# The first stage of a two-layer hybrid block written out for four queues

## The chip, the cores and the metric

One NeuronCore of a Trainium2 chip. Its engines work side by side and each takes its own instructions in order: TensorE (PE: matmuls, with weight loads shown apart as PEld), VectorE (DVE), ScalarE (ACT), GpSimd (POOL) and SyncE (SP), which here issues most transfers from memory. Engines wait for one another through semaphores. The metric is the device time of one execution in microseconds (us).

## The reference, cut to what matters

Two layers over 256 latent tokens `lat` and 256 context tokens `cx`, width 1024. The change touches only the first stage: the modulation of layer 0, the norm, and the first three of the 22 hidden blocks of its first feed-forward network, for both streams.

```python
def _rms(t, g):
    t32 = t.astype(jnp.float32)
    y = t32 * lax.rsqrt(jnp.mean(t32 * t32, axis=-1, keepdims=True) + NORM_EPS)
    return y.astype(t.dtype) * g

def _modulate(t, g, shift, scale):
    return _rms(t, g) * (1 + scale) + shift

def _swiglu(h, w13, w2):
    gte, up = jnp.split(h @ w13, 2, axis=-1)
    return (jax.nn.silu(gte) * up) @ w2
...
    mod = (jax.nn.silu(c) @ mod_w[i] + mod_b[i]).reshape(bsz, 3, 3, 1, D_MODEL)
    modc = (jax.nn.silu(c_ctx) @ mod_w[i] + mod_b[i]).reshape(3, 3, D_MODEL)
    lat = lat + 0.5 * mod[:, 0, 2] * _swiglu(_modulate(lat, norm_g[i, 0], mod[:, 0, 0], mod[:, 0, 1]), ffn_w13[i, 0], ffn_w2[i, 0])
    if cx is not None:
        cx = cx + 0.5 * modc[0, 2] * _swiglu(_modulate(cx, norm_g[i, 0], modc[0, 0], modc[0, 1]), ffn_w13[i, 0], ffn_w2[i, 0])
```

Behind it come a short convolution and a second feed-forward network in layer 0, and a feed-forward network, attention and another feed-forward network in layer 1.

## The kernel before

Activations lie transposed: 8 tiles `k` of 128 features on the partitions, 512 tokens along the row (256 latent tokens as stream `s=0`, 256 context tokens as `s=1`). Each fp32 product is made of three: both operands are split into a high part (`hi`, type fp32r, by an ACT copy) and a rest (`lo`, by a DVE subtraction), and `mm3` adds hi x hi, hi x lo and lo x hi in PSUM. So each weight costs TensorE three matmuls, ACT a copy and DVE a subtraction.

A hidden block of w13 is a raw tile of 1 MB (`wr`, three buffers, filled by SyncE's queue), whose first half holds the up columns and whose second half the gate columns. `w13_mm` multiplies it with the normalised input `h` into two PSUM tiles, `pg` and `pu`; `w13_post` makes silu(gate) x up. The stage makes blocks 0, 1 and 2 side by side in six PSUM tiles, because the input comes in pairs of tiles `q` = 0..3: the shift (`ch` 0, `B00`) and scale (`ch` 1, `A00`) of each pair hang on a 1 MB load of modulation weights each. Their steps:

- `P ch q`, `mod_pe`: the load (also into a `wr` buffer), eight matmuls of 32 columns, and a copy `row` out of PSUM;
- `T ch q`, `mod_turn`: two tiny matmuls turn the row onto partitions, and DVE adds the bias into `A00` or `B00`;
- `N q`, `norm_q`: for each tile and stream, x times scale over rms (`scaled`, L256, DVE), plus shift into `hh` (L266, ACT) and, in fp32, into `h32` (L271, ACT), and the rest `hl` (L267, DVE);
- `M i q`, `w13_mm` for block `i` and pair `q`: 12 matmuls of 512 columns;
- `W i`: load and split of block `i`; `F` and the products at the start (`fill`): matmuls whose results nobody reads.

Ahead of this, `square_add` squares each tile of x on ACT and adds it to one sum per stream on DVE, and `rms_inv` turns the sums into 1/rms by matmuls with ones, a square root, a reciprocal and a matmul that spreads it over the partitions.

The order of TensorE's instructions in the stage is written out as a string; the other queues follow the planner's order, which may pull later work in between:

```python
FIRST_STEPS = (
    "P10 P00 T10 T00 F W0 N0 W1 M00 W2 M10 P11 M20 P01 T11 T01 N1 M01 P12 M11 P02 T12 T02 N2 "
    "M21 P13 M02 P03 T13 T03 N3 M12 M22 M03 M13 M23 S"
)
```

`S` loads silu of the conditioning, `scbc`. With it DVE makes the remaining modulation from here on, one unit at a time (`mod_unit`, L142): a unit is a product with a sum over the row, four units (two where one stream is enough) to a 1 MB load, which sits in a `wr` buffer too. `tick` strews these units over the later stages. `h32` feeds sums of blocks of the input (`FirstBlocks.sums`), which from the ninth hidden block on save one product in eight. `hop` is a pool of 16 buffers of 4 KB per partition; `h` takes eight of them (`Plain`), the split block sums eight more later.

Of the kernel before, what the change touches and what calls it, by code (L numbers as in the profile page):

```python
# [25 lines left out]
HEADS = 8  # L26
KVH = 2
EPS = 1e-6
WARM = 36
FILL = 12  # L30

FIRST_STEPS = (
    "P10 P00 T10 T00 F W0 N0 W1 M00 W2 M10 P11 M20 P01 T11 T01 N1 M01 P12 M11 P02 T12 T02 N2 "
    "M21 P13 M02 P03 T13 T03 N3 M12 M22 M03 M13 M23 S"
)


@with_exitstack
def hybrid_kernel(ctx: ExitStack, tc: tile.TileContext, a: dict, out: bass.AP):
# [20 lines left out]
    def psmall(s="pq"):  # L63
        return pss.tile([P, T2], F32, tag="sm", name=nm(s))
# [18 lines left out]

    sccol = const.tile([P, KT, 32], F32, name="sccol", tag="sccol")
    nc.vector.memset(sccol, 0.0)
    nc.scalar.activation(out=sccol[:, :, :2], in_=ccol, func=AF.Silu)

    rowsum = cload("rowsum", [P, 2])
    scbc = mp.tile([P, 2, D], F32, name="scbc", tag="scbc", bufs=1)

# [74 lines left out]
    jobs += [(1, ch, p) for ch in range(9) for p in range(4)]  # L165
    units = []
    owed = [0.0]

    def next_unit():
# [117 lines left out]
    def pick(h, k, c0, c1):  # L287
        return h.at(k, c0, c1)
# [322 lines left out]
    def ffn(l, b, h, tot, gate, tail, gs=(), ev=1.5):  # L611
        gs = list(gs)
        i0 = 0
        for t, n in enumerate(THIRDS):
            between = ()
            if tot == T2:
# [22 lines left out]
                for i in range(len(gs), n):  # L639
                    if t == 0 and not heads and i in AS_IS[l, b]:  # L640
# [77 lines left out]

    h = Plain()
    h32 = {}  # L720
    idle = psmall("idle")
# [6 lines left out]
    fill(idle, WARM)  # L728
    for k in range(KT):
        square_add(k, 0, T2)  # L730
    ris = []
    for s in range(2):
        ris.append(tp.tile([P, S], F32, name=nm("ris"), tag=f"ris{s}", bufs=1))
        nc.scalar.copy(ris[s], rms_inv(s, (accs[s], accs[s, "last"])))
# [3 lines left out]
    nc.vector.tensor_scalar(  # L738
        out=sb1, in0=modb[:, 0, KT : 2 * KT], scalar1=1.0, scalar2=None, op0=ALU.add
    )  # L740

    def both(t):
        return t.unsqueeze(2).to_broadcast([P, 2, 2])

    rows = {}

    def mod_pe(ch, q):


        raw = load_raw(a["mod0"][ch, q])  # L750
        pr = psmall("pr")
        for k in range(KT):
            g = 32 * (k % 4)
            nc.tensor.matmul(
                pr[g : g + 32, :S], sccol[:, k, :], raw[:, k * S : k * S + S],
                start=(k < 4), stop=(k >= 4), tile_position=(0, g),
            )
        row = tp.tile([P, S], F32, name=nm("row"), tag="t", bufs=3)
        nc.scalar.copy(row, pr[:, :S])
        rows[ch, q] = pr, row  # L760

    def mod_turn(ch, q):

        pr, row = rows[ch, q]
        for j in range(2):
# [8 lines left out]
            in1=both(sb1[:, k2] if ch else modb[:, 0, k2]),  # L774
            op=ALU.add,
        )

    def norm_q(q):
        k2 = slice(2 * q, 2 * q + 2)
        nc.vector.tensor_tensor(  # L780
            out=A00[:, k2, :], in0=A00[:, k2, :], in1=both(normg[:, 0, 0, k2]), op=ALU.mult
        )
        for k in range(2 * q, 2 * q + 2):
            for s in range(2):
                if (q, s) not in h32:
                    h32[q, s] = gp.tile([P, T2], F32, name=nm("hr"), tag="gl" if s else "gh")
                norm_k(s, k, h, A00, B00, ris[s], h32[q, s][:, (k % 2) * S : (k % 2) * S + S])

    pps = [(psum("pg"), psum("pu")) for _ in range(3)]

    ws, gs0 = {}, []

    def load_sc():
# [4 lines left out]
    def first_w(i):  # L798
        if i < 2:
            ws[i] = load_w(a["w13"][0, 0, i], fine=True)  # L800
            return
        raw = load_raw(a["w13"][0, 0, i])
        parts = [new_pair("w") for _ in range(4)]
        for j in (0, 2, 1, 3):
            split(*parts[j], raw[:, j * T2 : j * T2 + T2])
        ws[i] = lambda o: tuple(t[:, o % T2 : o % T2 + P] for t in parts[o // T2])

    steps = {
        "P": mod_pe,
        "T": mod_turn,  # L810
        "F": lambda: fill(pps[2][0], FILL),
        "S": load_sc,
        "W": first_w,
        "N": norm_q,
        "M": lambda i, q: w13_mm(pps[i], ws[i], h, range(2 * q, 2 * q + 2), 0, T2),
    }
    with tc.manual_schedule(engines={mybir.EngineType.PE}):
        for step in FIRST_STEPS.split():
            steps[step[0]](*(int(c) for c in step[1:]))
# [7 lines left out]
    qg = cload("qg", [P, 1])  # L827
    kg = cload("kg", [P, 1])
    cosT = cload("cosT", [P, S])
    sinT = cload("sinT", [P, S])  # L830


    hn = Plain()
# [517 lines left out]
```

## Time and profile before

| | us |
|---|---|
| median of three runs | 1587.46 (1584.85 to 1589.65) |
| the profiled execution | 1589.78 |
| its span, first to last instruction | 1588.0 |
| TensorE busy, of the span | 1565.0 (99%) |
| VectorE busy | 1319.8 (83%) |
| ScalarE busy | 738.2 (46%) |
| mean granted TensorE clock | 0.995 |

An engine is busy while it executes; waiting at a semaphore is idle. A busy TensorE need not run at full pace: matmuls overlap, so the distance from start to start says more than the length of one. The granted clock is the share of full speed that TensorE was given. In a timeline a row says start, length, engine, line, operation, output and inputs, and in brackets the idle time ahead of it and what ended it. A group's row says how often, busy time and mean length in ns, and the idle time ahead.

### The profile page before, as it was taken

What the parts mean: (1) busy time and instruction counts of PE and PEld (TensorE: products, weight loads), DVE (VectorE), ACT (ScalarE), POOL (GpSimd) and SP (SyncE); (2) the same over time, 40 slices, a digit from 0 to 9 for tenths busy, and PEclk for the clock granted to TensorE, in tenths of its full rate; (3) what the DMA queues carried; (4) which work ended last, traced back from release to release, by engine and by line L of the source; (5) the groups of instructions that cost most, each with busy time, mean ns of one, the idle gap of its engine ahead of it and who ended that gap; (6) DMA issues with size and microseconds to landing.
All of it is one profiled execution on the core that took longest, in us unless ns stands there. A gap on an engine that the chain in (4) does not pass through costs nothing.

```text
span 1588.0 us, 25040 instructions
## 1 busy us (share of the span) xinstructions
PE 1565.0 (99%) x10210; PEld 1423.9 (90%) x10210; DVE 1319.8 (83%) x2029; ACT 738.2 (46%) x1180; POOL 29.8 (2%) x20
## 2 busy tenths in 40 slices
PE   8999999999999999999999999999999999899998
PEld 6788998998888899989899899899899898888887
DVE  5778778879998879799798899898898899976654
ACT  5532452544322356335345375335255455655543
POOL 0000000000000000000000000000000005200000
PEclk9999999999999999999999999999999999999999
DMA  8545234234565412452342423443433654645552
GB/s 319 181 174 201 92 115 167 104 117 162 186 214 193 177 65 95 142 200 104 130 177 102 160 103 107 158 161 107 175 133 122 235 186 149 234 156 186 186 202 90
DMA packets 38419, 248.74 MB, mean 157 GB/s; under 512 B 5280, under 2 KB 7072, under 8 KB 11936
## 3 DMA queue, kind: packets, MB, share of 16 engines
q1 hardware_dynamic: 35712, 245.38, 43.5%
q10 hardware_dynamic: 2592, 1.76, 0.4%
q8 instruction: 80, 1.31, 0.3%
q14 instruction: 35, 0.29, 0.1%
HBM read 244.77 MB, written 1.05 MB: 155 GB/s over the span
## 4 chain that ended last, share of the span: by engine, by line
PE 93%; DVE 3%; ACT 2%; DMA 1%; issue 1%; POOL 0%; DVEq 0%; POOLq 0%; ACTq 0%
PE py L122 9%; PE py L123 9%; PE py L124 9%; PE p L124 7%; PE p L123 7%; PE p L122 7%; PE q L122 5%; PE q L123 5%; PE q L124 5%; PE py L1107 3%; PE pg L1107 2%; PE pu L1107 2%; PE pg L122 2%; PE pg L123 1%; PE pg L124 1%; PE pu L124 1%
## 5 line engine op out<-in xcount | busy, mean ns | idle before, releaser
L98 ACT ACTIVATE wh<-wr 128x1024 fp32r<-128x1024 f32 (+2 forms) x276 | 277.2, 1015 | 352.2 <-PE py L123 81.2
L99 DVE TENSOR_TENSOR wl<-wr,wh 128x1024 fp32r<-128x1024 f32 (+2 forms) x276 | 319.7, 1166 | 78.4 <-ACT wh L98 71.0
L142 DVE CUSTOM_DVE_ANT_0 junk<-wr,scbc,modb 128x1024 bf16<-128x1024 f32 x224 | 286.8, 1280 | 25.0 <-DMA wr<-in_modT 22.2
L123 PE MATMUL py<-gl,wh 128*128 128x512 f32 (+1 forms) x570 | 213.3, 374 | 0.0
L122 PE MATMUL py<-gh,wh 128*128 128x512 f32 (+1 forms) x570 | 213.3, 374 | 0.0
L124 PE MATMUL py<-gh,wl 128*128 128x512 f32 (+1 forms) x570 | 213.0, 374 | 0.0
L99 DVE TENSOR_TENSOR wl<-ws,wh 128x1024 fp32r<-128x1024 f32 x108 | 131.3, 1223 | 28.6 <-ACT wh L98 28.1
L98 ACT ACTIVATE wh<-ws 128x1024 fp32r<-128x1024 f32 x108 | 113.4, 1058 | 75.1 <-DVE ws L563 32.5
L124 PEld LDWEIGHTS py<-gh,wl 128*128 128x128 f32 x570 | 107.3, 188 | 19.1
L122 PEld LDWEIGHTS py<-gh,wh 128*128 128x128 f32 x570 | 107.4, 188 | 18.5
L123 PEld LDWEIGHTS py<-gl,wh 128*128 128x128 f32 x570 | 107.4, 188 | 18.2
L123 PE MATMUL p<-tl,wh 128*128 128x256 f32 x432 | 122.2, 283 | 0.0
L124 PE MATMUL p<-th,wl 128*128 128x256 f32 x432 | 122.2, 283 | 0.0
L122 PE MATMUL p<-th,wh 128*128 128x256 f32 x432 | 122.2, 283 | 0.0
L122 PE MATMUL q<-bh,wh 128*128 128x256 f32 x320 | 90.6, 283 | 0.0
L123 PE MATMUL q<-bl,wh 128*128 128x256 f32 x320 | 90.6, 283 | 0.0
L124 PE MATMUL q<-bh,wl 128*128 128x256 f32 x320 | 90.6, 283 | 0.0
L122 PEld LDWEIGHTS p<-th,wh 128*128 128x128 f32 x432 | 82.9, 192 | 0.3
L123 PEld LDWEIGHTS p<-tl,wh 128*128 128x128 f32 x432 | 82.9, 192 | 0.3
L124 PEld LDWEIGHTS p<-th,wl 128*128 128x128 f32 x432 | 82.9, 192 | 0.0
L446 DVE SCALAR_TENSOR_TENSOR x<-py,G,x 128x256 f32<-128x256 f32 x144 | 62.9, 477 | 6.3 <-PE py L124 6.0
L557 DVE TENSOR_TENSOR ws<-wr 128x1024 f32<-128x1024 f32 x54 | 65.7, 1218 | 0.0
(296 smaller groups left out, 4181.1 us busy)
## 6 DMA issues: line engine op xcount, KB each, us to landing
wr<-in_w SPq DMA_DIRECT2D x88, 1024.0 KB, 4.9
wr<-in_modT SPq DMA_DIRECT2D x64, 1024.0 KB, 4.8
wr<-in_w2b SPq DMA_DIRECT2D x24, 896.0 KB, 4.6
wr<-in_w2a SPq DMA_DIRECT2D x12, 1024.0 KB, 4.8
wr<-in_mod SPq DMA_DIRECT2D x8, 1024.0 KB, 6.1
wr<-in_cw_cx SPq DMA_DIRECT2D x8, 1024.0 KB, 4.8
wr<-in_w2l SPq DMA_DIRECT2D x8, 1024.0 KB, 4.8
wr<-in_cw_b SPq DMA_DIRECT2D x4, 1024.0 KB, 4.9
```

The source lines that it names most:

```text
L98: nc.scalar.activation(out=hi, in_=src, func=AF.Copy)
L99: nc.vector.tensor_tensor(out=lo, in0=src, in1=hi.bitcast(F32), op=ALU.subtract)
L122: nc.tensor.matmul(ps, wh, mh, start=first, stop=False, **kw)
L123: nc.tensor.matmul(ps, wh, ml, start=False, stop=False, **kw)
L124: nc.tensor.matmul(ps, wl, mh, start=False, stop=last, **kw)
L142: nc.vector.tensor_tensor_reduce(out=junk, in0=raw[:, j * D : j * D + D], in1=scbc[:, v, :], scale=1.0, scalar=modb[:, l, col : col + 1], ...
L446: nc.vector.scalar_tensor_tensor(out=x[:, m, s * S : s * S + S], in0=ps[:, o : o + S], scalar=g[:, m, s : s + 1], in1=x[:, m, s * S : s * ...
L557: tt(out=sm.rearrange("p (a b c) -> p a b c", a=2, b=2)[:, :, 0, :], in0=a21.unsqueeze(1).to_broadcast([P, 2, T2]), in1=self.raw[:, T2 : 3 ...
L1107: nc.tensor.matmul(ps, w[0], m, start=first, stop=False, skip_group_check=True)
```

## The change

- **Sums of squares.** Squares are made whole (512 columns) by DVE (tiles 0, 1, 7) and ACT (2 to 6), added in pairs on DVE, and the four pair sums go to a PSUM tile by matmuls with ones. One square root serves both streams. Its activation table, and that of silu ahead of it, is called by a one-column activation (`table`) at the start.
- **x over rms ahead.** `over_rms` makes x/rms of a pair of tiles on DVE into `h32`, ahead of the modulation. `norm_q` then has one ACT operation per tile and stream (scale and shift into `hh`), and two on DVE (the same in fp32, in place, and the rest). The multiplication by the norm's gain moves to `mod_turn`.
- **Raw modulation in operand buffers.** A modulation load goes to two `hop` buffers, not to a `wr` buffer.
- **Weights in two pieces.** Of each block's load the first piece holds the columns for input tiles 0 and 1 (256 of 1024 in each half), the second the other six tiles.
- **Four queues.** The order of TensorE, DVE, ACT and SyncE in the stage is written out, step by step, and the loads are issued apart from their use. Per weight the two products with the high part of the input come first (`products`).
- The filling matmuls are 18 and 5, not 36 and 12. Modulation units and block sums are tied to stand behind the last subtraction of the norm (`issue_after`). Five small loads for later stages go to SyncE's queue.

```diff
-WARM = 36
-FILL = 12
+WARM = 18
+FILL = 5
...
-        mod_unit(*units.pop(0))
+        with tc.issue_after(begun[-1].ins):
+            mod_unit(*units.pop(0))
...
-                            h.sums()
+                            with tc.issue_after(begun[-1].ins):
+                                h.sums()
...
+    def ask_mod(ch, q):
+        raws[ch, q] = [hot("mr", F32) for _ in range(2)]
+        for j, t in enumerate(raws[ch, q]):
+            nc.sync.dma_start(t, a["mod0"][ch, q][:, j * 1024 : j * 1024 + 1024])
+
+    def ask_w(i, part):
+        if part == 0:
+            ws[i] = wp.tile([P, 2048], F32, name=nm("wr"), tag="wr", bufs=3)
+        c = slice(0, S) if part == 0 else slice(S, 1024)
+        nc.sync.dma_start(
+            ws[i].rearrange("p (h c) -> p h c", h=2)[:, :, c],
+            a["w13"][0, 0, i].rearrange("p (h c) -> p h c", h=2)[:, :, c],
+        )
...
+    def over_rms(q, ri):
+        for s in range(2):
+            t = h32[q, s] = gp.tile([P, T2], F32, name=nm("hr"), tag="gl" if s else "gh")
+            nc.vector.tensor_tensor(
+                out=t.rearrange("p (k t) -> p k t", k=2),
+                in0=x[:, 2 * q : 2 * q + 2, s * S : s * S + S],
+                in1=ri[:, s * S : s * S + S].unsqueeze(1).to_broadcast([P, 2, S]), op=ALU.mult,
+            )
 
     def norm_q(q):
...
+        for j in range(2):
+            k = 2 * q + j
             for s in range(2):
...
+                hh, hl = pick(h, k, s * S, s * S + S)
+                t = h32[q, s][:, j * S : j * S + S]
+                g, b = A00[:, k, s : s + 1], B00[:, k, s : s + 1]
+                nc.scalar.activation(out=hh, in_=t, func=AF.Identity, scale=g, bias=b)
+                nc.vector.tensor_scalar(
+                    out=t, in0=t, scalar1=g, scalar2=b, op0=ALU.mult, op1=ALU.add
+                )
+                begun.append(
+                    nc.vector.tensor_tensor(out=hl, in0=t, in1=hh.bitcast(F32), op=ALU.subtract)
+                )
...
+    with tc.manual_schedule(engines=ORDERED):
+        for ch, q in ((1, 0), (0, 0)):
+            ask_mod(ch, q)
+        for i in range(3):
+            ask_w(i, 0)
+        table(AF.Silu)
+        nc.scalar.activation(out=sccol[:, :, :2], in_=ccol, func=AF.Silu)
+        table(AF.Sqrt)
...
+        ps = psum("ss")
+        fill(idle, WARM)
+        for k, eng in enumerate((nc.vector, nc.vector) + (nc.scalar,) * 5 + (nc.vector,)):
+            square(k, eng)
+            if k % 2:
+                pair_sum(k // 2)
+                token_sums(ps, k // 2)
+        rs = tp.tile([P, 4], F32, name="rs4", tag="rs4", bufs=1)
+        nc.scalar.activation(out=rs, in_=ps[:, :4], func=AF.Sqrt, scale=1.0 / D, bias=eps_t)
+        nc.vector.reciprocal(rs, rs)
+        mod_pe(1, 0)
+        rb = psum("rb")
+        for i in range(4):
+            nc.tensor.matmul(
+                rb[:, i * P : i * P + P], rs[:, i : i + 1].to_broadcast([P, P]), ident,
+                start=True, stop=True,
+            )
+        over_rms(0, rb)
+        ris = tp.tile([P, T2], F32, name="ris", tag="gm", bufs=3)
+        nc.scalar.copy(ris, rb)
+        mod_pe(0, 0)
+        w_hi(0, 0)
+        w_lo(0, 0)
+        mod_turn(1, 0)
+        mod_turn(0, 0)
+        pps[0] = psum("pg"), psum("pu")
+        pps[1] = psum("pg"), psum("pu")
+        fill(pps[1][0], FILL)
+        norm_q(0)
+        for ch, q in ((1, 1), (0, 1)):
+            ask_mod(ch, q)
+        products(0, 0)
+        for i in (1, 2):
+            w_hi(i, 0)
+        w_lo(1, 0)
+        over_rms(1, ris)
+        w_lo(2, 0)
+        for i in range(3):
+            ask_w(i, 1)
+        mod_pe(1, 1)
+        mod_pe(0, 1)
+        for ch, q in ((1, 2), (0, 2)):
+            ask_mod(ch, q)
+        products(1, 0)
+        w_hi(0, 1)
+        w_lo(0, 1)
+        mod_turn(1, 1)
+        mod_turn(0, 1)
+        w_hi(1, 1)
+        norm_q(1)
+        products(2, 0)
+        products(0, 1)
+        w_hi(2, 1)
+        w_lo(1, 1)
+        over_rms(2, ris)
+        mod_pe(1, 2)
+        products(1, 1)
...
+        norm_q(3)
+        products(2, 2)
+        for i in range(3):
+            products(i, 3)
...
-    convk = cload("convk", [P, 3, KT])
+    convk = cload("convk", [P, 3, KT], nc.sync)
```

The steps left out for the third and fourth pair follow the same pattern: `mod_pe` for scale and shift between products of earlier pairs, their turns, `over_rms`, `norm_q`, then the pair's products.

More of the change, by code (lines that the diff above doesn't have):

```diff
@@ L28 @@
 EPS = 1e-6
-WARM = 36
-FILL = 12
[L35 to L38, printed above, removed]
+WARM = 18
+FILL = 5
+ORDERED = {
+    getattr(mybir.EngineType, e) for e in ("PE", "DVE", "Activation", "SP")
+}
 @with_exitstack
@@ L726, in fill, with table, both @@
             nc.tensor.matmul(ps[:, :P], ones, ones, start=True, stop=True)
[L728 to L734, printed above, removed]
+    def table(f):
+        t = const.tile([P, 1], F32, name=nm("table"), tag="ready")
+        nc.scalar.activation(out=t, in_=eps_t, func=f)
+    def both(t):
+        return t.unsqueeze(2).to_broadcast([P, 2, 2])
     A00 = const.tile([P, KT, 2], F32, name="A00", tag="A00")
@@ new lines, in products @@
+    def products(i, q):
+        if i not in pps:
+            pps[i] = psum("pg"), psum("pu")
+        for k in (2 * q, 2 * q + 1):
+            hh, hl = pick(h, k, 0, T2)
+            w = [w_at(i, (1 - j) * 1024 + k * P) for j in range(2)]
+            for n in range(3):
+                for j in range(2):
+                    nc.tensor.matmul(
+                        pps[i][j], w[j][n == 1], hl if n == 2 else hh,
+                        start=k == 0 and n == 0, stop=k == KT - 1 and n == 2,
+                    )
@@ L796, in load_sc @@
             nc.scalar.activation(out=scbc[:, v, :], in_=scbc[:, v, :], func=AF.Silu)
[L798 to L819, printed above, removed]
+    gs0 = []
     done[0, 0] = done[0, 1] = 16
```

102 lines of the change are left out of this document (77 added, 25 removed).

## The prediction, made before the run

> **What bounds the kernel now.** I read the page first, then the busy time by stretches, then the first 75 us as a timeline, with the waits of each queue beside it.
>
> ```profile
> span 1588.0 us, 25040 instructions
> PE 1565.0 (99%) x10210; PEld 1423.9 (90%) x10210; DVE 1319.8 (83%) x2029; ACT 738.2 (46%) x1180; POOL 29.8 (2%) x20
> ```
>
> TensorE is busy nearly all the time, so a change is worth what it saves on TensorE's own queue. But a busy TensorE is not one at full pace, so I asked for stretches: the opening, the rest of the first stage, and the stretch behind it (columns: length, busy time of the engines with their instruction counts, granted clock, DMA share, GB/s).
>
> ```profile
> 0.00:22.30 22.30, 20.23 (x160) 17.78 (x160) 8.76 (x30) 11.68 (x23) 0.19 (x4) 0.92 0.90 321
> 22.30:72.00 49.70, 46.91 (x267) 33.37 (x268) 33.07 (x68) 32.30 (x64) 0.00 (x0) 0.97 0.63 232
> 72.00:126.00 54.00, 54.00 (x240) 44.72 (x239) 40.25 (x56) 14.63 (x20) 0.00 (x0) 1.00 0.51 181
> ```
>
> In the second stretch TensorE idles 2.8 us, its weight loads run 33 us of 50, the clock is below full and the DMA engines are free for a third of the time. Behind 72 us nothing of that is left. The timeline gives the ends of the stage: its first product, and the first product of the fourth weight block.
>
> ```profile
> 22.31 0.50 PE L122 MATMUL pg<-hh,wh 128*128 128x512 f32 x1
> ...
> 70.12 0.39 PE L122 MATMUL pg<-hh,wh 128*128 128x512 f32 x1
> ...
> 71.48 0.39 PE L122 MATMUL pg<-hh,wh 128*128 128x512 f32 x1
> ```
>
> Between the last two rows stand six matmuls: 0.227 us each at full pace. The stage has 3 blocks x 8 tiles x 6 = 144 products, 32.7 us. The rest of its TensorE work after 22.31 is six modulation products (`mod_pe`) and three pairs of turns (`mod_turn`):
>
> ```profile
> 51.40 0.39 PE L124 MATMUL pu<-hh,wl 128*128 128x512 f32 x1
> 51.71 1.07 PE L754 MATMUL pr<-wr,sccol 128*32 128x256 f32 x16
> 52.71 0.50 PE L122 MATMUL pg<-hh,wh 128*128 128x512 f32 x1
> ...
> 55.38 0.39 PE L124 MATMUL pu<-hh,wl 128*128 128x512 f32 x1
> 55.70 1.07 PE L754 MATMUL pr<-wr,sccol 128*32 128x256 f32 x16
> 56.70 1.21 PE L766 MATMUL pr<-rowsum,row 128*128 128x2 f32 x8
> 57.77 0.48 PE L122 MATMUL pg<-hh,wh 128*128 128x512 f32 x1
> ```
>
> A lone `mod_pe` costs 52.71 - 51.40 - 0.23 = 1.1, with the slow first product behind it 1.2. With a pair of turns it is 57.77 - 55.38 - 0.23 = 2.15, with that product 2.25, so a pair of turns is 1.05. Six and three make 7.2 + 3.2 = 10.4. The floor from first product to last is then 43.1 us; the trace takes 71.48 - 22.31 = 49.2. **6.1 us are lost inside the stage.** Where:
>
> ```profile
> 30.87 5.17 DMA wr<-in_mod
> ```
>
> ```profile
> L122 PE MATMUL pg<-hh,wh 128*128 128x512 f32 x25 | 11.0, 442 | 2.6 <-ACT hh L266 2.5
> ```
>
> ```profile
> 34.60:38.00 3.40, 1.39 (x16) 1.06 (x9) 2.19 (x8) 1.74 (x5) 0.00 (x0) 1.00 0.97 407
> 38.00:41.40 3.40, 3.36 (x7) 2.37 (x8) 2.34 (x5) 1.93 (x5) 0.00 (x0) 0.50 0.98 372
> 41.40:44.80 3.40, 3.40 (x27) 2.10 (x27) 0.00 (x0) 0.87 (x2) 0.00 (x0) 0.99 0.21 83
> ```
>
> ```profile
> SPq L94 <- DVE wl L99: 28.8, 5, 12.3
> SPq L94 <- PE pr L754: 20.1, 5, 7.5
> ```
>
> The first fence is a piece of the chain of waits: a modulation load issued at 30.87 holds it up to 36. TensorE waits for the normalised operand that hangs on it (2.5 us over the stage; second fence, groups of 22.3 to 72) and then runs a stretch at half clock (third fence): 1.7 us lost, since 3.4 us at 0.50 do 1.7 us of work. That leaves 1.9, mostly in the first products, whose operands trickle in. The last fence (SyncE's queue, 22.3 to 72) says why the load was late: SyncE waits for one of the three `wr` buffers. From 41.4 DMA has nothing to do, 83 GB/s.
>
> **The change, part by part.** *Buffers and loads.* Modulation halves go to the 16 `hop` buffers, of which `Plain` holds 8; four modulation loads fit in the other 8. The three weight blocks own the three `wr` buffers. SyncE's 49 us of waits for buffers thus go. What is next late: the transfer itself. Two modulation loads of before show its pace (issue row, then issue to landing):
>
> ```profile
> 6.71 0.81 SPq L94 DMA_DIRECT2D wr<-in_mod  x2
> DMA to landing us min/median/max: 6.7/7.7/8.8
> ```
>
> They land at about 13.4 and 16.0: 2.6 us for 1 MB, 403 GB/s, close to the 407 and 372 above. In all 2.1 MB of x, 8.4 of modulation and 3.1 of weights come in. In the new order of issue their bytes give: first two modulation loads at 13.0 and 15.7, first weight pieces 16.4 to 18, second pair 23, second weight pieces 25, 27 and 29, the last modulation load at 40. Small pieces have no row here; at the opening's mean of 321 GB/s the 13.6 MB and a start at 2 end at 45, the later bound.
>
> *Opening chain.* The rows of before (timeline, then groups of 22.3 to 72):
>
> ```profile
> 9.98 1.28 ACT L220 ACTIVATE sq<-x 128x512 f32<-128x512 f32 x2
> 11.62 1.28 ACT L242 ACT_TABLE_LOAD   x1 [0.36 <-issue]
> ...
> 13.43 1.88 PE L248 MATMUL ss<-ident,ri 128*128 128x128 f32 x8
> 15.24 3.04 PE L754 MATMUL pr<-wr,sccol 128*32 128x256 f32 x32
> ...
> 17.24 0.37 ACT L759 COPY row<-pr 128x256 f32<-128x256 f32 x1 [1.52 <-PE pr L754]
> ```
>
> ```profile
> L98 ACT ACTIVATE th<-hr 128x512 fp32r<-128x512 f32 x8 | 4.5, 617 | 0.0
> ```
>
> ```profile
> L372 DVE TENSOR_TENSOR hr<-hr,hr 128x512 f32<-128x512 f32 x2 | 1.4, 692 | 0.0
> ```
>
> ```profile
> L266 ACT ACTIVATE hh<-t,mod 128x256 fp32r<-128x256 f32 x14 | 7.0, 497 | 4.0 <-DVE mod L771 4.0
> ```
>
> The last quarter of x is there at 9.98. Squares 6 and 7 now run side by side, a square and a pair sum by 0.69: 11.4; token sums, root (its table loaded ahead, where ACT waits for x) and reciprocal: 12.8. The first modulation load lets `mod_pe` start at 13.0; at half clock it takes 1.5 (half of 3.04): 14.5. Spreading the reciprocals (`rb`, as the 1.88 row): 16.4; the second `mod_pe` 17.9; row copy 0.37: 18.3. ACT then splits the first weight piece, two cuts of 256 columns at about 0.4 (row copy), DVE follows 0.4 later: 19.5. This is new in front of the modulation adds, which DVE has queued behind it; the three small adds 20.0; two operands on ACT by 0.5: **first product at 21.0 instead of 22.3, 1.3 earlier.** x over rms is two products of 0.69 on DVE, 16.4 to 17.8, under the second `mod_pe`; without that cover it costs 1.4.
>
> The table-load row says 1.28 us, of which I count 0.5 as saved, as the token sums ran beneath it. The Trainium skill, "ScalarE: Activation LUTs", section "What ACT_TABLE_LOAD costs", gives 2.66 us for a switch with its drain; by it the gain would be some 1.4 larger, but the root starts right behind the 1.28 here.
>
> *Norm.* Per tile and stream before: two ACT operations and two on DVE. Now one on ACT, two on DVE, one of them a scale-and-shift of 256 without a row; I take 0.3 (nearest: half of the 0.692 row, which has twice the columns and two tensors), bounds 0.15 and 0.5, times four per pair of tiles. ACT's `hh` has two pointers now: the 0.497 row to 0.6. It sits behind DVE's splits and `over_rms` in the written order, so I followed all queues through: with weights at 25, 27 and 29 the second norm starts behind its turns at 30, and its operands are there 2 us before their products; the third and fourth have 1 to 2 us. So inside the stage I put these at nothing: two other blocks' products (2.7 each) cover each. Without the cover a pair costs its 2 to 3 us.
>
> *Loads moved from ACT's queue to SyncE's* (`convk` to `sinT`): used hundreds of us later, nothing. *`issue_after`*: operand sums and modulation units may no longer enter DVE before the last norm; see the third case.
>
> *The clock.* Fewer filling products: 18 and 5 for 36 and 12. What idling does:
>
> ```profile
> 7.00:10.70 3.70, 3.68 (x33) 3.49 (x32) 3.44 (x11) 3.62 (x8) 0.00 (x0) 1.00 1.03 321
> 10.70:14.10 3.40, 2.51 (x21) 2.37 (x21) 1.50 (x6) 2.37 (x4) 0.00 (x0) 1.00 1.02 403
> 14.10:17.50 3.40, 3.40 (x29) 2.03 (x32) 0.00 (x0) 1.00 (x3) 0.00 (x0) 0.50 0.98 386
> ```
>
> A thinly used stretch is followed by one at 0.50, here and at 38.0. With the fill ending near 6.5 the half rate comes earlier in the opening, so I counted the opening at half clock; and another may fall on the first products. I take off 1.1 for two thirds of a stretch (0 to 3.4).
>
> **Sum.** 1.3 + 6.1 - 1.1 = 6.3 us earlier at the fourth block, and behind it TensorE is full, so it is kept. The profiled execution took 1589.78 (span 1588.0), 2.3 above the median; 1587.5 - 6.3 gives **1581**. About 0.3%, 4.8 us, is what a measurement of this kernel tells from no change.
>
> **Rivals.** *The clock and the opening eat it.* Were the opening no earlier and two stretches of the first products at half clock, 6.1 - 3.4 = 2.7 remain: 1585. For it: fewer fills, a longer written chain with in-order queues. Against: half clock never follows a full stretch. The Trainium skill, "TensorE: Matmul & The Clock Gate", Part 1, says the same: half rate after an idle window of about 3.4 us, windows running freely. By that rule this change loses at its thin opening; the rows agree (0.50 over 3.4 us, twice).
>
> *Slower: DVE behind the stage.*
>
> ```profile
> 70.00:80.00 10.00, 10.00 (x46) 8.29 (x45) 9.93 (x15) 3.45 (x5) 0.00 (x0) 1.00 0.51 179
> ```
>
> ```profile
> L99 DVE TENSOR_TENSOR tl<-hr,th 128x512 fp32r<-128x512 f32 x8 | 5.1, 682 | 0.0
> ```
>
> ```profile
> 75.39 1.21 DVE L99 TENSOR_TENSOR wl<-wr,wh 128x1024 fp32r<-128x1024 f32 x1
> 76.52 1.28 DVE L142 CUSTOM_DVE_ANT_0 junk<-wr,scbc,modb 128x1024 bf16<-128x1024 f32 x1
> ...
> 104.56 1.23 DVE L99 TENSOR_TENSOR wl<-wr,wh 128x1024 fp32r<-128x1024 f32 x1 [4.10 <-ACT wh L98]
> ```
>
> DVE is full after the stage (first row). Eight splits of operand sums (second) and eight sums of 0.69 ran before 72; now all wait for the last norm, and about half, some 5 us, is added to that backlog. The idle 4.1 at 104 and its like absorb it, if weight splits come first. If a load's four modulation units (5.2) stand ahead of a split that the next block needs, TensorE waits up to 5.2 per block, five blocks. Slower from the second block on (6.3 / 5.2), by over 0.3% from the third: 1581 + 15.6 = 1597. Against: at 75.39 the split stands before the units.
>
> *The change does not do what it says*, products still waiting for loads: at 240 GB/s the last load lands at 57 where 51 is wanted; no gain, 1587. The rows against: 321 to 407.
>
> **Numbers.** Forecast 0.60. The clock case 0.17 and the loads 0.08, both within 0.3%: 0.25. DVE 0.15. Range: 1576 (no half clock, the opening 2 us better, spread of the runs) to 1590, into the two middle cases; the DVE case lies outside.
>
> **What would show it.** First product near 21; the fourth block's first near 65; no SyncE waits on `wl` or `pr` in the stage; DMA full to 40; at most one half-clock stretch after the first product; TensorE full from 65 to 126. Wrong, if half clock reaches past 28, if TensorE waits for ACT `hh` over 1 us, or if weights of the fourth to eighth block are awaited.

## The result, and the profile after

| | before | after |
|---|---|---|
| median of 8 runs each, same chip (us) | 1587.36 (1584.85 to 1589.65) | 1581.99 (1578.61 to 1583.59) |
| the profiled execution (us) | 1589.78 | 1582.34 |
| its span (us) | 1588.0 | 1580.5 |
| first product of the stage | 22.31 | 21.82 |
| first product of the fourth block | 71.48 | 66.12 |

After over before is 0.9963, 95% interval 0.9952 to 0.9975: 5.4 us faster by the medians, where 6.3 were forecast. The two profiled spans differ by 7.5; of that, 5.4 stand at the fourth block, 5.2 at the first product with the second weights (`py`, 120.7 for 125.9), 5.0 at 1264 (its last product there, 1264.4 for 1269.4), and 7.5 at the end. The last 2 us come and go in stages that the change doesn't touch, and the medians don't have them: from that last product to the end the traces of all fourteen kernels here take between 315.0 and 318.6 us, without order by the edits.

The first line of the page of after and its engines' busy time:

```profile
span 1580.5 us, 24959 instructions
PE 1558.3 (99%) x10176; PEld 1422.0 (90%) x10176; DVE 1322.6 (84%) x2031; ACT 731.5 (46%) x1163; POOL 29.7 (2%) x20
```

6.7 of the 7.5 us by which the spans differ are gone from TensorE's busy time: a matmul at half clock is busy too. The stretches of after (length, busy time of PE, PEld, DVE, ACT, POOL with counts, granted clock, DMA share, GB/s):

```profile
6.40:9.80 3.40, 2.55 (x23) 2.36 (x22) 3.20 (x6) 2.58 (x6) 0.00 (x0) 1.00 1.01 324
9.80:13.20 3.40, 2.79 (x28) 2.69 (x31) 1.45 (x3) 0.63 (x1) 0.00 (x0) 1.00 1.01 387
13.20:16.60 3.40, 3.40 (x24) 2.17 (x24) 0.18 (x1) 0.64 (x2) 0.00 (x0) 0.50 1.07 362
16.60:20.00 3.40, 2.61 (x29) 1.82 (x28) 1.75 (x4) 1.48 (x4) 0.00 (x0) 0.99 0.88 254
20.00:23.40 3.40, 3.40 (x14) 2.88 (x13) 2.59 (x10) 2.72 (x7) 0.00 (x0) 0.51 0.99 253
...
24.40:40.00 15.60, 15.21 (x105) 10.77 (x104) 11.27 (x26) 7.91 (x15) 0.00 (x0) 1.00 1.02 404
40.00:66.00 26.00, 25.98 (x155) 19.63 (x154) 16.28 (x37) 13.60 (x22) 0.00 (x0) 1.00 0.46 189
66.00:126.00 60.00, 60.00 (x266) 49.53 (x265) 51.62 (x75) 21.88 (x31) 0.00 (x0) 1.00 0.50 178
```

The wait and the half-clock stretch between 34 and 41 are gone: from 24.4 on the clock is full and TensorE idles 0.4 us. DMA is full until 40. What is left of half clock lies in the opening (13.2 to 16.7) and on the first products (20.0 to 23.5). SyncE's waits from 22.3 to 72, and its timeline from 22 on:

```profile
SPq L91 <- DVE wl L96: 34.1, 2, 23.8
```

```profile
22.59 11.05 SPq L743 DMA_DIRECT2D mr<-in_mod  x8
34.54 1.61 SPq L970 DMA_DIRECT2D scbc<-in_c  x2
37.15 1.62 SPq L91 DMA_DIRECT2D wr<-in_w  x2
```

The last modulation loads go out in one run, and none waits for `pr`. SyncE still waits long for `wl`, but for the buffers of later blocks, behind every load of the stage. TensorE's timeline of after, from the token sums to the fifth block:

```profile
12.16 1.05 PE L797 MATMUL ss<-ones,sq 128*128 128x1 f32 x8 [0.61 <-DVE sq L793]
13.14 1.91 PE L810 MATMUL pr<-mr,sccol 128*32 128x256 f32 x16
...
16.85 1.07 PE L810 MATMUL pr<-mr,sccol 128*32 128x256 f32 x16
...
19.25 0.61 PE L822 MATMUL pr<-rowsum,row 128*128 128x2 f32 x4 [0.79 <-ACT row L815]
...
21.82 0.79 PE L870 MATMUL pg<-hh,wh 128*128 128x512 f32 x1
...
25.51 1.50 PE L810 MATMUL pr<-mr,sccol 128*32 128x256 f32 x24
27.40 0.64 PE L810 MATMUL pr<-mr,sccol 128*32 128x256 f32 x8 [0.39 <-DMA mr<-in_mod]
...
66.12 0.39 PE L119 MATMUL pg<-hh,wh 128*128 128x512 f32 x1
...
77.14 0.39 PE L119 MATMUL pg<-hh,wh 128*128 128x512 f32 x1
```

From first product to fourth block it is 44.3 us where the floor is 43.1. The first 12 products take 25.51 - 21.82 = 3.7 instead of 2.7 (half clock), and one modulation load is awaited for 0.39. Together these 1.4 are more than the loss of 1.2, so the floor was a little too high. And 49.2 - 44.3 = 4.9 of the 5.4 come from inside the stage, 0.5 from the opening.

### The profile page after: what moved, and what is told of

Same layout as the page of the kernel before. It is cut to its first block, busy times and chain, and to the rows that moved or that the text cites. A ratio compares the mean times of both kernels' runs of the same rounds, so it can differ in the third digit from the quotient of the medians.

```text
span 1580.5 us, 24959 instructions
## 1 busy us (share of the span) xinstructions
PE 1558.3 (99%) x10176; PEld 1422.0 (90%) x10176; DVE 1322.6 (84%) x2031; ACT 731.5 (46%) x1163; POOL 29.7 (2%) x20
## 3 DMA queue, kind: packets, MB, share of 16 engines
q8 instruction: 79, 1.29, 0.3%
HBM read 244.77 MB, written 1.05 MB: 156 GB/s over the span
## 4 chain that ended last, share of the span: by engine, by line
PE 92%; DVE 2%; DMA 2%; ACT 2%; issue 0%; POOL 0%; SPq 0%; ACTq 0%; DVEq 0%; POOLq 0%
PE py L119 9%; PE py L120 9%; PE py L121 9%; PE p L121 7%; PE p L120 7%; PE p L119 7%; PE q L119 5%; PE q L121 5%; PE q L120 5%; PE py L1260 3%; PE pg L1260 2%; PE pu L1260 2%; PE py L1261 1%; PE pg L121 1%; PE pu L121 1%; PE pg L119 1%
## 5 line engine op out<-in xcount | busy, mean ns | idle before, releaser
L95 ACT ACTIVATE wh<-wr 128x1024 fp32r<-128x1024 f32 (+2 forms) x264 | 270.6, 1033 | 340.3 <-PE py L120 85.1
L96 DVE TENSOR_TENSOR wl<-wr,wh 128x1024 fp32r<-128x1024 f32 (+2 forms) x264 | 312.4, 1189 | 71.0 <-ACT wh L95 63.5
## 6 DMA issues: line engine op xcount, KB each, us to landing
mr<-in_mod SPq DMA_DIRECT2D x16, 512.0 KB, 10.2
```

The costliest lines, as they stand in the source:

```text
L95: nc.scalar.activation(out=hi, in_=src, func=AF.Copy)
L96: nc.vector.tensor_tensor(out=lo, in0=src, in1=hi.bitcast(F32), op=ALU.subtract)
```

## Experiments

Each was timed in five rounds against the kernel before on the same chip, whose median was 1588.14 us beside the first four kernels, 1587.94 beside the next four and 1587.57 beside the last four; across these groups the ratios are compared (0.001 is 1.6 us), not the medians. The first two rows repeat the result. The "4th block" is its first product in that kernel's trace. "Half clock" gives the stretches of the first 75 us, in steps of 0.1 us, in which that trace shows a granted clock of about 0.5. The expectations name their theories by letters; where a letter matters, the text says what it stands for.

| kernel | median us | ratio to before (95%) | first product | 4th block | half clock |
|---|---|---|---|---|---|
| before | 1587.36 | 1 | 22.31 | 71.48 | 14.1 to 17.6, 38.0 to 41.5 |
| after | 1581.99 | 0.9963 (0.9952 to 0.9975) | 21.82 | 66.12 | 13.2 to 16.7, 20.0 to 23.5 |
| buffers only | 1588.87 | 1.0007 (0.9999 to 1.0016) | 21.66 | 72.57 | 37.2 to 44.1 |
| order only | 1588.19 | 0.9999 (0.9987 to 1.0011) | 22.17 | 72.67 | 33.7 to 40.6 |
| buffers and order | 1584.69 | 0.9980 (0.9970 to 0.9991) | 21.86 | 67.84 | none |
| two loads ahead | 1583.00 | 0.9965 (0.9951 to 0.9979) | 21.60 | 65.02 | 11.1 to 18.1 |
| weights whole | 1585.46 | 0.9984 (0.9974 to 0.9995) | 21.84 | 68.37 | 11.8 to 18.7, 22.1 to 25.6 |
| late small loads | 1581.72 | 0.9967 (0.9957 to 0.9977) | 22.27 | 65.90 | 10.2 to 17.1, 20.4 to 23.9 |
| opening reordered | 1580.61 | 0.9956 (0.9944 to 0.9968) | 21.67 | 65.10 | 11.5 to 18.5 |
| fills as before | 1584.35 | 0.9980 (0.9969 to 0.9990) | 23.55 | 66.47 | 16.3 to 19.8 |
| no table calls | 1582.94 | 0.9968 (0.9957 to 0.9979) | 21.91 | 65.33 | 12.0 to 19.0 |
| no tie | 1582.16 | 0.9967 (0.9954 to 0.9980) | 22.16 | 65.54 | 10.9 to 17.9 |
| DVE loaded | 1591.40 | 1.0025 (1.0014 to 1.0035) | 23.29 | 66.66 | 12.6 to 19.6 |
| opening and late small loads | 1580.42 | 0.9956 (0.9942 to 0.9970) | 21.31 | 64.74 | 10.9 to 17.8 |

Each place in a trace is that of one execution. After, two loads ahead, no tie and DVE loaded have the same opening, and their first products lie between 21.60 and 23.29; so a first product that is some tenths of a us earlier shows nothing by itself. The time from the first product to the fourth block is steadier.

**Buffers only.** The prediction put the wait at 36 down to the shared `wr` buffers. So the kernel before, with nothing but its modulation loads moved:

```diff
-        raw = load_raw(a["mod0"][ch, q])
+        raw = [hot("mr", F32) for _ in range(2)]
+        for j, t in enumerate(raw):
+            nc.sync.dma_start(t, a["mod0"][ch, q][:, j * 1024 : j * 1024 + 1024])
...
```

> The kernel before with one edit: a raw modulation load goes to two operand buffers, not to a weight buffer. Theory A (three shared buffers held the loads back, and that is most of the gain): the modulation wait at 36 (2.0 us) and the half-clock stretch behind it (1.7 us) go, the fourth block's first product comes at about 67.8 instead of 71.5, the median falls by 3.7 us to about 1583.7. Rival B (the written order of the queues makes the gain, more buffers alone do not): the fourth block stays at 71 or later, the median within 1 us of 1587.4.

Nothing was gained. TensorE's timeline of this kernel, then ACT's:

```profile
37.91 0.79 PE L122 MATMUL pg<-hh,wh 128*128 128x512 f32 x1 [2.96 <-ACT hh L266]
```

```profile
34.32 1.28 ACT L798 ACT_TABLE_LOAD   x1
35.61 1.06 ACT L798 ACTIVATE scbc<-scbc 128x1024 f32<-128x1024 f32 x1
36.57 0.49 ACT L266 ACTIVATE hh<-t,mod 128x256 fp32r<-128x256 f32 x1
```

The loads were early and SyncE's waits on `pr` gone, and TensorE still waited 2.96 for `hh`. With the loads out of the way the planner pulled the silu of the conditioning, with its table load, ahead of `hh`. That cost about 1.0 of the 2.96: the shift was ready at 35.57 (a DVE row of 35.42, 0.15 us long), and `hh` began at 36.57. But even without that the norm could not have been ready, as DVE's timeline of before shows:

```profile
35.48 0.16 DVE L771 TENSOR_TENSOR A<-pr,sb 128x4 f32<-128x4 f32 x1 [4.63 <-PE pr L766]
36.04 0.48 DVE L256 SCALAR_TENSOR_TENSOR t<-x,A,ris 128x256 f32<-128x256 f32 x1 [0.20 <-DMA wr<-in_mod]
```

The chain of waits of before names the load for 5.17 us, yet the idle time that ended with it is 0.20. What came last are the turns, then three steps (add, scale, `hh`) while TensorE has nothing left: in the old string `T11 T01 N1` are followed at once by `M01`, which needs them.

**Order only, and both together.** So the second theory: the wait is the latency of the norm behind its turns. One edit of the string puts another block's products there; the second kernel has both edits.

```diff
-    "... M10 P11 M20 P01 T11 T01 N1 M01 ..."
+    "... M10 P11 P01 T11 T01 N1 M20 M01 ..."
```

> The kernel before with TensorE's written order alone changed at one place: the third block's first products (M20) stand behind the second pair's turns, so that they cover the norm. New theory F (the wait at 36 was the norm's latency with nothing of TensorE behind the turns, and the loads' lateness stood hidden below it: order and buffers are needed together): P01 moves ahead of M20, from 33.8 to about 31, where its load is not there before 33.5; the wait moves there, the fourth block's first product stays at 71 to 72, median 1587 to 1588. Rival G (order is the whole of it): 68, median 1584.

> The kernel before with that order and the raw modulation in operand buffers. Theory F: the loads are early (in the run with buffers alone both land before 30) and the norm lies under M20; the wait of 2 to 3 us and the half-clock stretch (1.7 us) go, the fourth block's first product comes at 67.0 to 68.5 instead of 71.5, median 1583.5 to 1584.5, two thirds of the whole change. Rival H (neither counts; the gain of the change comes from ACT's and DVE's written order): 70 or later, median above 1586.

Order alone gains nothing either; its TensorE timeline shows the wait one step earlier, now at the load, and its stretch from 34 to 42 the half clock:

```profile
33.17 1.41 PE L754 MATMUL pr<-wr,sccol 128*32 128x256 f32 x16 [2.42 <-DMA wr<-in_mod]
```

```profile
34.00:42.00 8.00, 8.00 (x32) 6.31 (x25) 4.53 (x12) 3.68 (x9) 0.00 (x0) 0.59 0.91 356
```

The same stretch with the buffers only:

```profile
34.00:42.00 8.00, 5.04 (x17) 3.77 (x17) 4.61 (x12) 6.77 (x12) 0.00 (x0) 0.70 1.03 413
```

With both, the timeline and the same stretch read:

```profile
30.85 0.64 PE L756 MATMUL pr<-mr,sccol 128*32 128x256 f32 x8 [0.35 <-DMA mr<-in_mod]
...
36.30 0.50 PE L123 MATMUL pg<-hl,wh 128*128 128x512 f32 x1 [0.21 <-DVE hl L267]
```

```profile
34.00:42.00 8.00, 7.68 (x43) 5.03 (x42) 2.99 (x7) 4.86 (x11) 0.00 (x0) 1.00 1.03 410
```

Two waits lay one upon the other: singly 0.7 and 0.2 us above before (both within the measurement), together 3.2 below. That is the larger half of the change's 5.4, and it is shown. The clock makes it look sharper than the waits alone: behind its wait each single edit runs at half clock for 6.9 us, before for 3.5, and both together not at all. The longer stretch costs up to 1.7 us; less that, each alone would start the fourth block at about 70.9, some 0.5 ahead of before (an estimate from the table), and both together start it 3.6 ahead. Whether a single edit always has the longer stretch, one trace of each doesn't show. The rest, 67.84 to 66.12, can be read from the two traces and was not run by itself: with both edits the first 24 products take 29.00 - 21.86 = 7.1 us where 24 x 0.227 is 5.4, as `hh`, weights and their rests trickle in; in after 12 products go first, then the modulation products, and the next 12 don't stall.

**Two loads ahead.** Is it the depth of four loads that counts? Here four `hop` buffers of after are held idle until the last scale add, so that only two modulation loads fit.

```diff
+    held = [hot("held", F32) for _ in range(4)]
+    for t in held:
+        nc.gpsimd.memset(t[:, :2], 0.0)
...
+    for t in held:
+        nc.gpsimd.tensor_copy(out=t[:, :2], in_=A00[:, KT - 1, :])
```

> The changed kernel with four of the sixteen operand buffers held by an idle tile until the last modulation add, so that two modulation loads fit at a time, not four. Theory A': what counts is that modulation no longer competes with weights for buffers, not the depth; loads of the third pair are asked for at about 27 and land by 33 to 36, where 38 is needed: the fourth block's first product moves by less than 1 us from 66.1, median 1582 to 1583. Rival C (depth carries the gain): modulation is awaited again, 3 us or more lost, median 1585 or more.

The fourth block starts at 65.02 and the ratio is that of the change within its interval. Depth is worth nothing that these intervals show: two loads ahead that don't wait for a weight are enough.

**Weights whole.** After, with each block's 1 MB in one transfer at the first place:

```diff
-        c = slice(0, S) if part == 0 else slice(S, 1024)
-        nc.sync.dma_start(
...
+        if part == 0:
+            nc.sync.dma_start(ws[i], a["w13"][0, 0, i])
```

> The changed kernel with each weight block loaded whole at the place of its first piece. Theory A: 2.4 MB more stand ahead of the second pair of modulation loads, which land about 5.5 us later, at 30 and 33, where TensorE wants them at 25.5; 5 to 7 us are lost (the wait, and a half-clock stretch after it), the fourth block's first product comes at 71 to 73, median 1587 to 1589, the gain is gone. Rival D (the pieces do not matter, the order absorbs it): within 1 us of 1582.

```profile
28.54 0.64 PE L807 MATMUL pr<-mr,sccol 128*32 128x256 f32 x8 [0.73 <-DMA mr<-in_mod]
29.72 0.64 PE L807 MATMUL pr<-mr,sccol 128*32 128x256 f32 x8 [0.55 <-DMA mr<-in_mod]
```

The second pair of modulation loads comes behind 3 MB of weights and is awaited twice in this timeline, 1.3 us in all; the fourth block is 2.25 later, and the ratio 0.0021 or 3.3 us above the change's. Some 0.7 of the 2.25 is the clock, as the half-clock stretch on the first products (22.1 to 25.6) costs 1.7 where that of after costs 1.0. The two pieces are worth some 2 to 3 us, less than the 5 to 7 expected.

**Late small loads.** In after, five small loads went out on SyncE from 11.15 on, ahead of the second pair of modulation loads, in SyncE's timeline:

```profile
11.15 0.60 SPq L67 DMA_DIRECT2D convk<-in_convk  x1
...
15.73 0.33 SPq L67 DMA_DIRECT2D sinT<-in_sinT  x1
16.48 2.72 SPq L743 DMA_DIRECT2D mr<-in_mod  x4
```

```diff
+            last = nc.sync.dma_start(scbc[:, v, :], a["c2"][v : v + 1, :].to_broadcast([P, D]))
...
+    with tc.issue_after(last.ins):
+        convk = cload("convk", [P, 3, KT], nc.sync)
...
```

> The changed kernel with the five small loads for later stages tied behind the last load of the stage on SyncE's queue; in the trace of the change they stand ahead of the second pair of modulation loads, from 11.15 to 16.06. Theory E (they hold those loads back): the second pair is asked for from about 11.5, lands 1.5 to 2 us earlier, the 0.4 us wait of TensorE on it goes, the fourth block's first product comes at 65.5 to 65.8; median 0.3 to 0.8 us lower, too little for the time, seen in the profile. Rival: no change in the stage, 66.1.

```profile
25.95 1.93 PE L810 MATMUL pr<-mr,sccol 128*32 128x256 f32 x32
```

In the timeline the 32 matmuls of that pair now run through: the 0.39 is gone. But so they do in four kernels that keep the small loads where after has them (two loads ahead, opening reordered, no table calls, no tie), so the 0.39 belongs to one trace. What the place of the small loads does is to bring the pair's last landing from 27.4 (issued at 18.8, 8.6 us) to 23.1 (13.7, 9.4 us): with them in front it comes just in time. In the ratio (0.9967 for 0.9963) nothing of it can be seen.

**Opening reordered.** Why was the first product at 21.82 and not 21.0? Two rows of DVE's timeline of after, and two of ACT's:

```profile
16.96 1.29 DVE L841 TENSOR_TENSOR hr<-x,rb 128x512 f32<-128x512 f32 x2 [3.23 <-PE rb L906]
...
19.54 0.76 DVE L777 TENSOR_TENSOR wl<-wr,wh 128x256 fp32r<-128x256 f32 x2 [1.30 <-ACT wh L773]
```

```profile
18.33 0.58 ACT L912 COPY ris<-rb 128x512 f32<-128x512 f32 x1 [2.86 <-DVE hr L841]
18.81 0.38 ACT L815 COPY row<-pr 128x256 f32<-128x256 f32 x1
```

ACT's copy of the spread reciprocals, which is not needed before the second pair, stands in the written order ahead of the second row copy, and starts only when DVE has read the same PSUM tile. So the row copy that the turns need starts at 18.81, though its matmuls (16.85, 1.07 us long) end at 17.92. And the modulation adds stand behind the subtraction of weights at 19.54.

```diff
         over_rms(0, rb)
-        nc.scalar.copy(ris, rb)
         mod_pe(0, 0)
         w_hi(0, 0)
-        w_lo(0, 0)
         mod_turn(1, 0)
         mod_turn(0, 0)
+        w_lo(0, 0)
...
         products(0, 0)
+        nc.scalar.copy(ris, rb)
```

> The changed kernel with two pieces of its opening reordered: ACT's copy of the spread reciprocals stands behind the first norm, not ahead of the copy of the second modulation row (which waited for it from 17.9 to 18.8), and DVE makes the modulation adds ahead of the first weight piece's subtraction. Theory I (my figure of the opening missed by these two): the first product comes at 20.5 instead of 21.8, the fourth block's at 64.9 instead of 66.1, median 1580.5 to 1581. Rival (the subtraction or the half clock is waited for instead): first product 21 or later, fourth block 66.

```profile
12.08 1.87 PE L797 MATMUL ss<-ones,sq 128*128 128x1 f32 x8 [0.61 <-DVE sq L793]
...
21.67 0.50 PE L870 MATMUL pg<-hh,wh 128*128 128x512 f32 x1 [0.23 <-ACT hh L854]
```

The fourth block starts 1.0 earlier, but the first product only 0.15, not 1.3. In this trace the half clock runs from 11.5 to 18.5, over the token sums (1.87 us for the 1.05 of after) and the first modulation products, and the first products ran at full pace (0.50 for 0.79). The second `mod_pe` starts 0.89 later than in after and ends 1.2 later, at 19.1; from its end to the first product it is 2.6 us for 3.9. So the two pieces gained 1.3 there, as expected, what the half clock took ahead of them ate it, and the products got it back.

**Fills as before.** `WARM` 36 and `FILL` 12 in after.

> The changed kernel with the filling products of before, 36 and 12. Theory J: the fills at the start keep the clock full to about 14 as before, and the first products are at full clock (0.9 us in their first four), but twelve fills in front of the first product end at 22.3 at full clock, or at 24.8 at half, so the first product is 0.5 to 3 later; the fourth block's first product comes at 65.5 to 68, median 1581.5 to 1584. Rival (the clock gate alone decides): 65.2, median 1581.

```profile
1.03 10.70 PE L725 MATMUL idle<-ones 128*128 128x128 f32 x72 [1.03 <-DVE eps_t L81]
11.57 3.63 PE L797 MATMUL ss<-ones,sq 128*128 128x1 f32 x32
...
23.55 0.48 PE L870 MATMUL pg<-hh,wh 128*128 128x512 f32 x1
```

36 fills hold TensorE's queue until 11.57, and all token sums stand behind them; the first product is 1.7 later. The products then run at full clock, the fourth block stands 42.9 behind the first product for 44.3, and so it is only 0.35 later than in after. The ratio is 0.0017 or 2.7 us above the change's, but the two intervals overlap, and the trace has the rest behind 1264, in stages that no edit touches. That smaller fills are worth more than the 0.35 is not shown.

**No table calls.** After without the two `table` lines.

> The changed kernel without the two calls that load activation tables ahead; silu's table then loads when its input has landed at 5.2, and the root's ahead of the root. My figure was 0.5 us for the root's load, as token sums run beneath it; here only the last quarter's sums (1 us) do, so 0.3 to 1.3 us later, the first product at 22.1 to 23.1, fourth block 66.4 to 67.4, median 1582 to 1583.5. By the price of a switch with its drain (2.66 us, from the Trainium skill, ScalarE: Activation LUTs, What ACT_TABLE_LOAD costs) the root would be 1.7 to 2.7 later, first product 23.5 to 24.5, median 1583.5 to 1584.7.

```profile
10.73 1.28 ACT L899 ACT_TABLE_LOAD   x1
...
13.14 0.26 ACT L899 ACTIVATE rs<-ss,eps_t 128x4 f32<-128x4 f32 x1 [1.13 <-PE ss L797]
```

ACT's timeline: the root's table is loaded under the last sums, and the root still waits 1.13 for TensorE. The calls ahead save nothing that can be measured. The Trainium skill, "ScalarE: Activation LUTs", "What ACT_TABLE_LOAD costs", gives 2.66 us for a switch with its drain. Here the load itself took 1.28, and what it may cost beyond that would lie hidden in the 1.13 us of waiting behind it. In the kernel before nothing is hidden: its load ends at 12.90 (11.62 and 1.28), its root starts at 12.91, and only 0.36 us of idling stands ahead of the load.

**No tie.** After without both `issue_after` of the change.

> The changed kernel without the ties: block sums and modulation units may enter DVE's queue before the last norm again. Theory K (DVE behind the stage has slack, as TensorE is full from 66 on): some sums run inside the stage, where DVE idles, and nothing is gained by it; fourth block's first product within 0.5 us of 66.1, median 1581 to 1583. Rival (the backlog behind the stage costs): 1 us or more faster, below 1581.

The tie gains nothing and costs nothing that these intervals show: 0.9967 for 0.9963.

**DVE loaded.** The slower rival was a DVE backlog behind the stage. To see how much DVE can still take, each of the eight splits of block sums has its subtraction done three times, 16 x 0.6 = 9.6 us more on DVE and nothing else:

```diff
                 split(hi[:, c], lo[:, c], src)
+                for _ in range(2):
+                    nc.vector.tensor_tensor(
+                        out=lo[:, c], in0=src, in1=hi[:, c].bitcast(F32), op=ALU.subtract
+                    )
```

> The changed kernel with each of the eight splits of the block sums done three times by DVE (the same values again): 16 subtractions of 0.6 us, 9.6 us more of DVE work in the backlog behind the stage. Theory K: the weight splits stand ahead of it or are early enough, modulation units move back, TensorE stays full from 66 to 126; median within 1.5 us of 1582. The slower case of the prediction: a split that a block needs stands behind the backlog and TensorE waits, 3 to 9 us, median 1585 to 1591.

I expected slack to take most of it, and it took none: 0.0062 or 9.8 us above the change. TensorE's timeline and DVE's:

```profile
79.56 0.50 PE L119 MATMUL pg<-hh,wh 128*128 128x512 f32 x1 [0.82 <-ACT wh L95]
...
86.49 0.80 PE L121 MATMUL pu<-hh,wl 128*128 128x512 f32 x1 [5.74 <-DVE wl L96]
```

```profile
82.21 2.49 DVE L366 TENSOR_TENSOR tl<-hr,th 128x512 fp32r<-128x512 f32 x4
...
85.22 1.22 DVE L96 TENSOR_TENSOR wl<-wr,wh 128x1024 fp32r<-128x1024 f32 x1
```

The sums' splits stand ahead of the fifth block's second weight split, and TensorE waits 0.82 and 5.74 for that block's operands; its clock from 84 to 90 is 0.53, some 1.7 us of the 3.5 that it is busy there, and the half clock lasts to 91.2, another 0.6. With the 0.5 by which the fourth block is later (66.66) these make 9.4 of the 9.8. In after the margin is small, on DVE's timeline:

```profile
73.05 1.90 DVE L96 TENSOR_TENSOR tl<-hr,th 128x512 fp32r<-128x512 f32 x3
74.86 2.37 DVE L96 TENSOR_TENSOR wl<-wr,wh 128x1024 fp32r<-128x1024 f32 x2
```

Those two weight splits end at 77.23, and the block that needs them starts at 77.14. The second split's first product is the sixth of the block, 5 x 0.227 = 1.1 us on, at about 78.3: it is ready a microsecond ahead.

**Opening and late small loads.** The two edits that the traces suggest, together in after.

> The changed kernel with the reordered opening and the five small loads behind the stage's loads, together. Each alone brought the fourth block's first product from 66.1 to 65.1 and 65.9. Theory: they overlap partly (the loads no longer late for the earlier products), 64.8 to 65.1, median 1580 to 1581, under 2 us better than the change. Rival: the half-clock stretch falls on the first products again and takes back 0.9, 65.9, median 1581.5.

1580.42 us, the fourth block at 64.74, the earliest of all. It is 0.1% below the change, and the intervals overlap: no worse, and not shown to be better.

## Why the prediction was right

The forecast was 1581 and the median is 1581.99, faster by 0.37%. Point by point:

- *The loss inside the stage, 6.1 less 1.1 for the clock*: 4.9 came of a forecast 5.0. **This sum held and one of its reasons didn't.** The prediction read the 2.5 us wait for `hh` as the fault of the shared buffers, from the chain of waits. Buffers alone gain nothing; the norm's latency in TensorE's written order stood just beneath. The prediction had both remedies in its sum, the buffers as the cause and the other blocks' products only as a cover for the new norm ("two other blocks' products cover each"). Had the change been the buffers alone, the same reasoning would have forecast up to 4 us and been wrong.
- *The opening, 1.3*: 0.5 in the trace of after, the term that was mis-sized, and with the spread of first products between traces of one opening even the 0.5 is not firm. In that trace the chain is on time until the second `mod_pe` ends (17.92, forecast 17.9). Missed was the copy `ris`, which waits for DVE's read of the same PSUM tile and has the row copy behind it (0.9). Of the 0.5 counted for the table load nothing shows: without the calls ahead the first product comes at 21.91 for 21.82.
- *The clock, 1.1*: about 1.0 on the first 12 products. It ended at 23.5, well before the 28 set as the mark, and each half stretch of after follows one in which TensorE was busy 2.6 to 2.8 of 3.4 us. The prediction's "half clock never follows a full stretch" fell: with the order only, TensorE is busy for all of 33.7 to 37.1 at half clock, and the half clock goes on to 40.6. By the Trainium skill's rule ("TensorE: Matmul & The Clock Gate", Part 1: half rate after an idle window, windows running freely) where it falls is partly chance. The traces agree in that its place differs, and differ in that the stretch ahead was thin and not idle. What the place is worth can be read from the table. In six kernels with the change (two loads ahead, opening reordered, no table calls, no tie, DVE loaded, opening and late small loads) all half clock lies ahead of the first product, and from there to the fourth block it is 43.4 us in each; in after, with half clock on the first products, it is 44.3. The rest of the spread of the fourth block (64.7 to 66.7) stands in the opening. Whether it is chance from one execution to the next, no run shows, as each kernel has one trace.
- *Scale-and-shift on DVE, 0.3 (0.15 to 0.5)*: 0.41, inside the stage hidden as said. `hh` 0.59, where 0.60 was said. The groups of after, 24 to 60:

```profile
L854 ACT ACTIVATE hh<-hr,mod,A 128x256 fp32r<-128x256 f32 x12 | 6.2, 590 | 1.9 <-DVE mod L827 1.9
...
L855 DVE TENSOR_SCALAR hr<-hr,A,mod 128x256 f32<-128x256 f32 x13 | 5.3, 409 | 1.7 <-ACT hh L854 1.7
```

- *Small loads on SyncE, nothing*: right in size, with a reason that doesn't hold. "Used hundreds of us later" is none: the planner issued them at 11 to 16, ahead of loads that were due, and these then land only as TensorE asks for them. The 0.39 us awaited in the trace of after is not there in four others.
- *DVE behind the stage*: TensorE waits for nothing from 66 to 126, as forecast, but not because of slack. The idle 4.1 at 104 was to absorb the backlog "if weight splits come first", and that condition fails: with the sums' splits ahead of a weight split, 9.6 us more cost 9.8. The rival's mechanism is real, with the sums' splits in place of its modulation units, and the change stays on the good side of it by about a microsecond at the fifth block. The price of 5.2 per block, over five blocks, was not seen: one block paid, and the rest of DVE's lag didn't come back.
- The tie, the depth of four loads and the table calls are each worth nothing measurable; the written order with separate buffers (3.2) and the two pieces of weights (2 to 3 if taken back) are what the change is shown to live on, and what the smaller fills are worth stays open. These don't add up to 5.4, as the pieces were taken back from a kernel that has the others. The sums of squares on two engines and x over rms ahead were not taken back by themselves.

## What to carry to other kernels

The releaser that a chain of waits names is what came last, not all that was late. Look at the idle time that ended with it (0.20 us here, beside 5.17 on the chain) and at what the next product would have waited for anyway; two faults that lie on each other show little until both are taken away. Where an in-order queue is written out by hand, ask of each instruction who stands behind it: an early copy of 0.58 us that waits for another reader held the next one up for 0.9 us, sum splits of 9.6 us ahead of a weight split cost 9.8, and small loads ahead of due ones left those just in time. And a busy share of 84% says nothing about slack: at one place DVE had a microsecond.

## What was not expected of the hardware

- Two engines reading one PSUM tile did not read it side by side in this kernel: the matmuls that fill `rb` ended at 16.92, DVE's two reads ran from 16.96 for 1.29 us, and ACT's copy began as they ended, at 18.33. So 1.4 of the 2.86 us that ACT stood idle were a wait for the other reader. Whether the chip or the order of the semaphores makes it so was not tried.
- Busy time alone doesn't say what keeps the clock up. In after 2.55 busy us of 3.4 (6.4 to 9.8, filling products and token sums) are followed by full clock, and 2.79 (9.8 to 13.2, token sums alone, one column wide) by half clock. In the first 100 us of all fourteen traces a half-clock stretch is 3.5 or about 7 us long, nothing between. What decides was not tried.
- A second per-partition pointer costs ACT some 0.1 us on 256 columns (590 ns for the 497 before), and the fp32 scale-and-shift of DVE takes 0.41 us, well above half of the 0.69 that its operations on two tensors of 512 take.
